# Gate products of the first branch placed among query projections, last heads and SSD preparation; second branch placed in recurrence and pooling

## The chip, the cores and the metric

The kernel runs on one core of a Trainium2 chip. The metric is the device time of one execution in microseconds. One more execution of the kernel was recorded by the hardware profiler; every row of a trace below is from it.

TensorE (PE) multiplies; a product of 128x128 weights with 512 columns is one matmul instruction. VectorE (DVE) and ScalarE (ACT) work element by element and read PSUM, where the products land. GpSimd (POOL) works element by element in SBUF. SyncE (SP) issues nearly all DMAs. The profile gives the granted clock of TensorE as a share of its 2.4 GHz level; 0.50 is the 1.2 GHz level.

## The reference, cut to what matters

One layer, 512 tokens, width 1024. Four mixers read the same normalised hidden state; the output of each goes through its own weights and is gated by a product of the hidden state.

```python
h = rmsnorm(x, g_mix[l])
u = h @ w_in[l]
c_q, c_kv, k_r, u_pool, z, xbc, dt, lru_g, lru_x, gates = jnp.split(u, pts, axis=-1)
y_a = mla_mixer(c_q, c_kv, k_r, cos, sin, ...)       # 8 heads, rotary part shared by the heads
y_b = pool_mixer(u_pool, w_pool[l], pool_scale[l])   # causal windows of 2, 4, 8, 16
y_c = ssd_mixer(z, xbc, dt, ...)                     # chunks of 128 tokens
y_d = rglru_mixer(lru_g, lru_x, ...)                 # recurrence over tokens
gates = jax.nn.sigmoid(gates.reshape(b, s, N_BRANCH, D_MODEL))
merged = (gates[:, :, 0] * (y_a @ w_branch[l, 0]) + gates[:, :, 1] * (y_b @ w_branch[l, 1])
          + gates[:, :, 2] * (y_c @ w_branch[l, 2]) + gates[:, :, 3] * (y_d @ w_branch[l, 3]))
x = x + merged @ w_out[l]
x = x + jnp.square(jax.nn.relu(rmsnorm(x, g_mlp[l]) @ w_ff1[l])) @ w_ff2[l]
x = x + (p[l] @ w_ple[l]) * jax.nn.sigmoid(rmsnorm(x, g_ple[l]) @ w_ple_gate[l])
return rmsnorm(x, g_final)
```

The four branches are called 0 (attention), 1 (pooling), 2 (SSD) and 3 (recurrence).

## The kernel before

**Products.** Every operand is split into a rounded part and a rest (`split`, `split_scaled`), and each product is three matmuls with float32r operands (`mm3`, lines 199 to 202). A projection (`proj`, line 292) of 8 blocks is 24 matmuls into one PSUM tile of tag m, of which there are three buffers. A product with a branch's own weights has 4 blocks, 12 matmuls.

**Weights.** They come in units, in the order of the list `UNITS` (lines 53 to 116): SP loads 128x1024 numbers, ACT makes the rounded part `wh` (line 169), DVE the rest `wl` (line 170). `unit()` keeps two units ahead; there are two raw and three split buffers.

**Order.** The kernel is written in program order, and a planner that simulates the engines while the program is built makes from it the instruction list of each engine. Program order is the priority; an instruction that the planner takes to be ready may be placed ahead of others. On the chip every engine works its list strictly in order. A tile has a tag with a fixed number of buffers (line 122: G1, G2, G3 16 each, T1 6, T2 8, T3 6, Z 4, X 8), and a new tile of a tag waits until an old one has been read for the last time.

**Stages around the change, in program order:**

- Line 431: a projection for the rotary key and dt, then three units of query weights (lines 443 to 452). Two of the six query tiles hold the rotary parts; `rotate` (line 421) reads such a PSUM tile six times on DVE, and writes two heads, the second by an addition on POOL (line 429). The others are copied by ACT (`head_pair`).
- Lines 453 to 467: key and value projections; lines 456 to 458 make eight masked copies of the rotated key.
- Lines 516 to 558: attention, one head per turn, the scores of the next head beside the weighting of this one. `split_head` (line 494) splits a head's key and query into four T1 tiles, the rounded part on ACT, the rest on POOL. After each of the first six heads stands one xBC projection (`xbc_tile`, line 483).
- Lines 561 to 578: `branch(n, j)` is gate product, tanh on ACT, product with the branch's weights, one DVE instruction, and for all branches but the first an addition on POOL into `merged[j]`. The tanh of the first branch lies in G3, of the others in T2.
- Lines 581 to 701: SSD. `branch(0, c)` stands after each of four chunks (line 689).
- Lines 717 to 741: four turns of the recurrence, `branch(0, 4 + i)` in each (line 722). Lines 747 to 758: four gelu turns. Lines 764 to 784: four pooling turns, in which POOL adds shifted copies and a matmul (line 783) mixes the result.
- Lines 789 to 796: branches 2, 1 and 3, eight times each; after branch 1 the residual x is loaded again (line 795). Then `merged` is split and the output projection follows (line 802).

Of the kernel before, what the change touches and what calls it, by code (L numbers as in the profile page):

```python
# [10 lines left out]
F32 = mybir.dt.float32  # L11
F32R = mybir.dt.float32r
# [5 lines left out]
P = 128  # L18
S = 512
# [37 lines left out]
def _unit(key, width):  # L57
    UIDX[key] = len(UNITS)
    UNITS.append((key, width))
# [4 lines left out]
for _i in range(4):  # L64
    _unit(("z", _i), 1024)
_unit(("krdt", 0), 576)
for _i in range(3):
    _unit(("uq", _i), 768)
_unit(("uk", 0), 1024)
_unit(("uv", 0), 1024)  # L70
for _i in (4, 5, 0, 1, 2, 3):
    _unit(("xbc", _i), 1024)
BR_ORDER = (0, 2, 1, 3)

UQ_ORDER = ((1, 0), (0, 0), (1, 1), (1, 2), (0, 1), (1, 3))


def _branch_units(n, j):
    _unit(("gate", n, j), 1024)
    if j % 2 == 0:  # L80
        _unit(("br", n, j // 2), 1024)


for _i in range(8):
    if _i >= 4:
        _unit(("lx", _i - 4), 1024)
    _branch_units(BR_ORDER[0], _i)
for _i in range(4):
    _unit(("lg", _i), 1024)
for _i in range(4):  # L90
    _unit(("pool", _i), 1024)
for _n in BR_ORDER[1:]:
    for _j in range(8):
        _branch_units(_n, _j)
for _i in range(8):
# [23 lines left out]
def trunk(tc, xT, pT, pos, par_d, cst_d, gfin, wblk_d, wpool_d, W, out, dbg=None):  # L119
# [4 lines left out]
    with ExitStack() as ctx:  # L124
# [12 lines left out]
        def A(tag, dt=F32, n="a"):  # L137
            return ap_.tile([P, S], dt, name=nm(n), tag=tag, bufs=TAGS[tag])
# [271 lines left out]
            zs.append(a)  # L410


        qh = [A("G1", F32, "qraw") for _ in range(H)]
        kh = [A("G1", F32, "kraw") for _ in range(H)]

# [5 lines left out]
        def rotate(ps, r0, dst, dst2=None):  # L421
            tmp, tmc = A("T3", F32, "rot"), A("T3", F32, "roc")
            m = r0 + 32
            dve.tensor_tensor(out=tmc[64:, :], in0=ps[r0:r0 + 64, :], in1=cosT[r0:r0 + 64, :], op=ALU.mult)
            dve.tensor_tensor(out=tmp[64:96, :], in0=ps[m:m + 32, :], in1=sinS[m:m + 32, :], op=ALU.mult)
            dve.tensor_tensor(out=tmp[96:, :], in0=ps[r0:m, :], in1=sinS[r0:m, :], op=ALU.mult)
            dve.tensor_tensor(out=dst[64:, :], in0=tmc[64:, :], in1=tmp[64:, :], op=ALU.add)
            if dst2 is not None:
                pool.tensor_tensor(out=dst2[64:, :], in0=tmc[64:, :], in1=tmp[64:, :], op=ALU.add)

        w = unit("krdt", 0)
        ps = proj(w, hh, KD, stride=72, m=72)
# [5 lines left out]
        for t in range(NT):  # L438
            pe.transpose(out=ps[:, t * 8:(t + 1) * 8], in_=kd[64:72, t * P:(t + 1) * P], identity=ident[64:72, 64:72])
        dtr = SM(32, "dtr")  # L440
        dve.tensor_tensor(out=heads(dtr, 8), in0=heads(ps[:, 0:32], 8),
                          in1=pc("dtb", 0, 8).unsqueeze(1).to_broadcast([P, NT, 8]), op=ALU.add)
        for u in range(3):
            w = unit("uq", u)
            for v in range(2):
                ps = proj(w, cq, 3, off=v * 384)
                a, i = UQ_ORDER[2 * u + v]
                if a:
                    head_pair(ps, i, qh)
                else:  # L450
                    for p in (2 * i, 2 * i + 1):
                        rotate(ps, (p % 2) * 64, qh[2 * p], qh[2 * p + 1])
        w = unit("uk", 0)
        for i in range(4):
            head_pair(proj(w, ckv, 2, off=i * 256), i, kh)
        for hd in range(H):
            dve.tensor_scalar(out=kh[hd][64:, :], in0=kro[64:, :], scalar1=cc("half", hd % 2, 1)[64:, :],
                              scalar2=None, op0=ALU.mult)
        w = unit("uv", 0)
        vv = []  # L460
        for t in range(NT):
# [29 lines left out]

        def split_head(src):
            h, l = A("T1", F32R, "hdh"), A("T1", F32R, "hdl")
            act.copy(out=h, in_=src)
            pool.tensor_tensor(out=l, in0=src, in1=h.bitcast(F32), op=ALU.subtract)
            return h, l

        def scores(q, k, qt):  # L500
            n = (qt + 1) * P
# [12 lines left out]
            return sm  # L514

        ya = []
        k_ = split_head(kh[0])
        q_ = split_head(qh[0])
        pr = [scores(q_, k_, qt) for qt in range(NT)]
        for hd in range(H):  # L520
            nxt = []
            po = PS("o")
            if hd + 1 < H:
                k_ = split_head(kh[hd + 1])
                q_ = split_head(qh[hd + 1])
            def weighted(kt, h, l):
                ro = (hd % 2) * 64
                vs = slice(hd * 64 - ro, hd * 64 + 64)
# [19 lines left out]
            pr = nxt  # L548
            if hd < 6:
                xbc_tile((4, 5, 0, 1, 2, 3)[hd])  # L550
            if hd % 2 == 0:
                yh, yl = A("G3", F32R, "yah"), A("G3", F32R, "yal")
                act.copy(out=yh[:64, :], in_=po[:64, :])
                dve.tensor_tensor(out=yl[:64, :], in0=po[:64, :], in1=yh[:64, :].bitcast(F32), op=ALU.subtract)
                ya.append((yh, yl))
            else:
                act.copy(out=yh[64:, :], in_=po[64:, :])
                dve.tensor_tensor(out=yl[64:, :], in0=po[64:, :], in1=yh[64:, :].bitcast(F32), op=ALU.subtract)


        yall = {0: ya}
        merged = [None] * 8
        bws = {}

        def branch(n, j):
            gw = unit("gate", n, j)
            if j % 2 == 0:
                bws[n] = unit("br", n, j // 2)
            pg = proj(gw, hh, KD)
            first = n == BR_ORDER[0]  # L570
            th = A("G3" if first else "T2", F32, "gth")
            act.activation(out=th, in_=pg, func=AF.Tanh, scale=0.5)
            pb = proj(bws[n], yall[n], 4, off=(j % 2) * S)
            dve.scalar_tensor_tensor(out=th, in0=th, scalar=1.0, in1=pb, op0=ALU.add, op1=ALU.mult)  # L574
            if first:
                merged[j] = th
            else:
                pool.tensor_tensor(out=merged[j], in0=merged[j], in1=th, op=ALU.add)  # L578


        dt = softplus(dtr, 32)
# [33 lines left out]
        for c in range(NT):  # L615
            ps = PS("t")
            for i in range(4):
                pe.transpose(out=ps[:, i * P:(i + 1) * P], in_=xbc[i][:, csl(c)], identity=ident)
            xt = A("T1", F32, "xt")
            act.copy(out=xt, in_=ps)  # L620
            xdt.append(A("G1", F32, "xdt"))
            xsd.append(A("G1", F32, "xsd"))
            dve.tensor_tensor(out=heads(xdt[c]), in0=heads(xt), in1=bc8(dt[:, c8(c)]), op=ALU.mult)
            pool.tensor_tensor(out=heads(xsd[c]), in0=heads(xt), in1=bc8(pc("dsk", 0, 8)), op=ALU.mult)
        btall = A("T1", F32, "bt")
        ps = PS("t")
        for c in range(NT - 1):
# [3 lines left out]
        for g in range(2):  # L631
            ps = PS("s")
            gs = slice(g * 64, g * 64 + 64)
            for c in range(NT):
                pe.matmul(ps[:, csl(c)], lhsT=xbc[4][gs, csl(c)], rhs=xbc[5][gs, csl(c)], start=True, stop=True)
            dve.tensor_tensor(out=heads(cbm[g], P), in0=heads(ps, P), in1=U.unsqueeze(1).to_broadcast([P, NT, P]),
                              op=ALU.mult)
        for c in range(NT):
            for g in range(2):
                e = A("G1", F32, "E")  # L640
# [3 lines left out]
                for j in range(4):  # L644
# [3 lines left out]
                pool.tensor_tensor(out=heads(e, P), in0=heads(e, P),  # L648
                                   in1=cbm[g][:, csl(c)].unsqueeze(1).to_broadcast([P, 4, P]), op=ALU.mult)
                G.append(e)  # L650

        R = [None]
        for c in range(NT - 1):
# [16 lines left out]
        for c in range(NT):  # L670
# [15 lines left out]
                dve.tensor_tensor(out=xsd[c], in0=y, in1=xsd[c], op=ALU.add)  # L686
            dve.tensor_tensor(out=zs[c], in0=xsd[c], in1=zs[c], op=ALU.mult)
            act.activation(out=y, in_=zs[c], func=AF.Square, accum_out=yssq[:, c:c + 1])
            branch(BR_ORDER[0], c)
        v = SM(NT, "v")  # L690
        dve.tensor_scalar(out=v, in0=yssq, scalar1=1.0 / (4 * 512), scalar2=EPS, op0=ALU.mult, op1=ALU.add)
        f = rsqrt(v, NT)
# [4 lines left out]
        for i in range(4):  # L697
            ps = PS("t")
            for c in range(NT):
                pe.transpose(out=ps[:, c * P:(c + 1) * P], in_=zs[c][:, i * P:(i + 1) * P], identity=ident)  # L700
            yc.append(split_scaled(ps, pc("snorm", i), "G1", "yc"))


        wba, wbi = A("T3", F32, "wba"), A("T3", F32, "wbi")
# [12 lines left out]
        for i in range(4):  # L717
            w = unit("lx", i)
            ps = proj(w, hh, KD)
            xc, e = A("G1", F32, "xc"), A("G1", F32, "le")  # L720
            conv(ps, lcw, pc("lcb", 0, 4), 4, i, xc)
            branch(BR_ORDER[0], 4 + i)
            pa, pi = PS("s"), PS("s")
            pe.matmul(pa, lhsT=wba[:, i * P:(i + 1) * P], rhs=xc, start=True, stop=True)
            pe.matmul(pi, lhsT=wbi[:, i * P:(i + 1) * P], rhs=xc, start=True, stop=True)
# [21 lines left out]
        for i in range(4):  # L747
# [7 lines left out]
            act.activation(out=t, in_=t, func=AF.Tanh, scale=GELU_C)  # L755
            dve.scalar_tensor_tensor(out=t, in0=t, scalar=1.0, in1=g, op0=ALU.add, op1=ALU.mult)
            dve.tensor_tensor(out=t, in0=t, in1=lus[i], op=ALU.mult)
            yd.append(split_scaled(t, 0.25, "G1", "yd"))


        wpl = A("T3", F32, "wpl")
        sync.dma_start(out=wpl, in_=wpool_d)
        yb = []
        for i in range(4):
            w = unit("pool", i)
            ps = proj(w, hh, KD)
# [12 lines left out]
                                     op0=ALU.mult, op1=ALU.subtract)  # L779
            dve.tensor_tensor(out=a[:, :n], in0=src[:, :n], in1=cc("rc", i * 16, n), op=ALU.mult)  # L780
            dve.tensor_tensor(out=a[:, :n], in0=a[:, :n], in1=u[:, :n], op=ALU.subtract)
            ps = PS("t")
            pe.matmul(ps, lhsT=wpl[:, i * P:(i + 1) * P], rhs=a, start=True, stop=True)
            yb.append(split_scaled(ps, pc("psc", i), "X", "yb"))

        yall.update({1: yb, 2: yc, 3: yd})


        for n in BR_ORDER[1:]:
            for j in range(8):  # L790
                branch(n, j)
            if n == 1:
                xres = [A("X", F32, "x") for _ in range(KD)]
                for k in range(KD):
                    sync.dma_start(out=xres[k], in_=xT[:, k, :])
        mg = [split_scaled(m, 0.5, "G1", "mg") for m in merged]


        def residual_in(g):
# [335 lines left out]
```

## Time and profile before

| | |
|---|---|
| median of 3 runs | 1002.74 us (1002.37 to 1002.94) |
| the profiled execution | 1005.16 us, of which its span 1003.1 us |
| busy in the span | PE 966.5 us, DVE 666.1, ACT 485.4, POOL 171.3 |
| mean granted TensorE clock | 0.989 |
| DMA | 96.97 MB, mean 97 GB/s |

Read first the busy times, then the same by stage with the granted clock, then what TensorE waited for, and last the timelines around the longest waits. A matmul's duration in the trace overlaps with the next; the distance from start to start is what it costs.

### The profile page before, as it was taken

Reading aid. Unit: us, or ns where it says so; the run is one execution under the profiler, and the core shown is the slowest. Engines: PE = TensorE matmul, PEld = TensorE weight load, DVE = VectorE, ACT = ScalarE, POOL = GpSimd, SP = SyncE. Lnnn points to the kernel's source line nnn. Section 1 sums busy time; section 2 is a strip of 40 time slices with the busy share of each in tenths; the row PEclk is TensorE's granted clock in tenths of the full one; section 3 lists DMA queues with packets and bytes.
Section 4 is the critical chain, followed back from the end, with each engine's and each line's share of the span. In section 5 each row is a group of like instructions: output and inputs, shape, how many; then the busy total and the mean of one; then the engine's idle time right before and its main releaser. Section 6 shows DMA issues by size and latency. Waiting matters only on the chain. (4 is left out here: it accounts for less than half of the span.)

```text
span 1003.1 us, 12054 instructions
## 1 busy us (share of the span) xinstructions
PE 966.5 (96%) x4389; PEld 787.6 (79%) x4389; DVE 666.1 (66%) x1140; ACT 485.4 (48%) x856; POOL 171.3 (17%) x127
## 2 busy tenths in 40 slices
PE   7997999899999899999999999999999999999996
PEld 5776788687777678888888888778887887888785
DVE  7769776657676743434342655897788689689636
ACT  6746786755367432222232434453543453466633
POOL 0003221133004351111121000423005005000021
PEclk9998999999999899999999999999999999999998
DMA  5422121042113223232532334433213404424002
GB/s 196 133 69 85 64 71 56 22 148 85 64 63 105 95 81 109 84 105 84 189 106 85 105 110 146 144 116 125 84 59 121 155 13 126 154 77 147 1 1 84
DMA packets 36475, 96.97 MB, mean 97 GB/s; under 512 B 4768, under 2 KB 4800, under 8 KB 36416
## 3 DMA queue, kind: packets, MB, share of 16 engines
q1 hardware_dynamic: 35472, 95.35, 28.9%
q10 hardware_dynamic: 944, 0.85, 0.3%
q8 instruction: 34, 0.56, 0.2%
q14 instruction: 25, 0.20, 0.1%
HBM read 94.01 MB, written 2.18 MB: 96 GB/s over the span
## 5 line engine op out<-in xcount | busy, mean ns | idle before, releaser
L170 DVE TENSOR_TENSOR wl<-wr,wh 128x1024 fp32r<-128x1024 f32 (+3 forms) x126 | 162.3, 1291 | 149.8 <-ACT wh L169 148.3
L169 ACT CAST wh<-wr 128x1024 fp32r<-128x1024 f32 (+3 forms) x126 | 128.7, 1023 | 251.9 <-PE psm L201 164.6
L200 PE MATMUL psm<-hh,wh 128*128 128x512 f32 (+1 forms) x408 | 163.5, 401 | 0.0
L201 PE MATMUL psm<-hl,wh 128*128 128x512 f32 (+1 forms) x408 | 161.4, 396 | 0.0
L202 PE MATMUL psm<-hh,wl 128*128 128x512 f32 (+1 forms) x408 | 160.7, 394 | 0.0
L202 PE MATMUL psm<-x2h,wl 128*128 128x512 f32 x256 | 100.0, 391 | 0.9 <-DVE wl L170 0.9
L200 PE MATMUL psm<-x2h,wh 128*128 128x512 f32 x256 | 99.9, 390 | 0.0
L201 PE MATMUL psm<-x2l,wh 128*128 128x512 f32 x256 | 99.9, 390 | 0.0
L201 PEld LDWEIGHTS psm<-hl,wh 128*128 128x128 f32 (+1 forms) x408 | 76.9, 188 | 18.3 <-issue 2.4
L200 PEld LDWEIGHTS psm<-hh,wh 128*128 128x128 f32 (+1 forms) x408 | 76.7, 188 | 18.5 <-issue 2.3
L202 PEld LDWEIGHTS psm<-hh,wl 128*128 128x128 f32 (+1 forms) x408 | 76.8, 188 | 18.0 <-issue 1.7
L185 DVE TENSOR_TENSOR wl<-b,wh 128x512 fp32r<-128x512 f32 x96 | 81.8, 898 | 2.5 <-ACT wh L184 2.5
L184 ACT CAST wh<-b 128x512 fp32r<-128x512 f32 x96 | 54.4, 618 | 56.0 <-PE pss L202 30.4
L865 POOL TENSOR_TENSOR t<-b,b 128x512 f32<-128x512 f32 x16 | 26.9, 1691 | 238.5 <-DVE xtok L856 136.4
L578 POOL TENSOR_TENSOR gth<-gth,gth 128x512 f32<-128x512 f32 x24 | 34.9, 1453 | 158.1 <-DVE gth L574 158.1
L202 PEld LDWEIGHTS psm<-x2h,wl 128*128 128x128 f32 x256 | 48.1, 188 | 11.6 <-DVE wl L170 1.8
L200 PEld LDWEIGHTS psm<-x2h,wh 128*128 128x128 f32 x256 | 48.1, 188 | 9.9
L201 PEld LDWEIGHTS psm<-x2l,wh 128*128 128x128 f32 x256 | 48.1, 188 | 9.8
L883 DVE SCALAR_TENSOR_TENSOR ffr<-psm,bc 128x512 f32<-128x512 f32 x32 | 21.9, 688 | 35.3 <-PE psm L202 32.1
L574 DVE SCALAR_TENSOR_TENSOR gth<-gth,psm 128x512 f32<-128x512 f32 x32 | 22.0, 687 | 16.2 <-PE psm L202 15.9
L987 POOL TENSOR_TENSOR xtok<-xtok,gf 128x512 f32<-128x512 f32 x7 | 9.0, 1290 | 134.1 <-ACT pth L986 134.1
L200 PE MATMUL psm<-pgh,xph 128*128 128x512 f32 (+1 forms) x72 | 26.6, 370 | 0.8 <-ACT xph L940 0.8
(398 smaller groups left out, 2105.4 us busy)
## 6 DMA issues: line engine op xcount, KB each, us to landing
wr<-W SPq DMA_DIRECT2D x114, 512.0 KB, 3.3
b<-W SPq DMA_DIRECT2D x64, 256.0 KB, 3.4
pgw<-W SPq DMA_DIRECT2D x16, 256.0 KB, 2.9
x<-xT SPq DMA_DIRECT2D x15, 256.0 KB, 6.6
wr<-W SPq DMA_DIRECT2D x8, 320.0 KB, 4.3
E<-acd SPq DMA_DIRECT2D x8, 256.0 KB, 6.2
out<-xtok SPq DMA_DIRECT2D x8, 256.0 KB, 2.3
wr<-W SPq DMA_DIRECT2D x3, 384.0 KB, 2.9
```

The costliest lines, as they stand in the source:

```text
L169: act.copy(out=hi[:, :n], in_=raw[:, :n])
L170: dve.tensor_tensor(out=lo[:, :n], in0=raw[:, :n], in1=hi[:, :n].bitcast(F32), op=ALU.subtract)
L184: act.copy(out=hi[:, c], in_=src)
L185: dve.tensor_tensor(out=lo[:, c], in0=src, in1=hi[:, c].bitcast(F32), op=ALU.subtract)
L200: pe.matmul(ps, lhsT=s_h, rhs=m_h, start=first, stop=False, **kw)
L201: pe.matmul(ps, lhsT=s_h, rhs=m_l, start=False, stop=False, **kw)
L202: pe.matmul(ps, lhsT=s_l, rhs=m_h, start=False, stop=last, **kw)
L574: dve.scalar_tensor_tensor(out=th, in0=th, scalar=1.0, in1=pb, op0=ALU.add, op1=ALU.mult)
L578: pool.tensor_tensor(out=merged[j], in0=merged[j], in1=th, op=ALU.add)
L865: pool.tensor_tensor(out=t1, in0=b12, in1=b11, op=ALU.subtract)
L883: dve.scalar_tensor_tensor(out=r, in0=ps, scalar=0.0, in1=rb, op0=ALU.max, op1=ALU.mult)
L987: (dve if last else pool).tensor_tensor(out=xt[t][hf][:, c], in0=xt[t][hf][:, c], in1=gf[:, hf, c], op=ALU.mult)
```

## The change

The first branch is taken apart into its gate product (`gate`) and the product with its weights (`project`). Gates (0,0) and (0,1) stand among the query projections, (0,2) and (0,3) after the last two heads, (0,4) behind the attention, (0,5) to (0,7) in the SSD preparation; their tanh lies in X or G1, not in G3. The SSD chunks keep the eight products. Branch 2 is spread over the recurrence, gelu and pooling turns (`MIXED`), and branch 3 goes ahead of branch 1. The rotation's second sum becomes a copy on ACT; a head's rest parts are made on DVE, and the masked key copy with them, head by head. The pooling matmul stands one turn later. x is loaded again after the split of `merged`. Other tags change to make room. The list of units follows the new order.

```diff
-for _i in range(3):
-    _unit(("uq", _i), 768)
+_unit(("gate", 0, 0), 1024)
+_unit(("uq", 0), 768)
+_unit(("uq", 1), 768)
+_unit(("gate", 0, 1), 1024)
+_unit(("uq", 2), 768)
...
-BR_ORDER = (0, 2, 1, 3)
+BR_ORDER = (0, 2, 3, 1)
...
+MIXED = {"lx": ((), (), (0,), (1,)), "lg": ((2,), (3,), (4,), (5,)), "pool": ((), (6,), (), (7,))}
...
+        yall = {}
+        merged = [None] * 8
+        gts, bws = {}, {}
+
+        def gate(n, j, tag="T2"):
+            pg = proj(unit("gate", n, j), hh, KD)
+            gts[n, j] = th = A(tag, F32, "gth")
+            act.activation(out=th, in_=pg, func=AF.Tanh, scale=0.5)
+
+        def project(n, j):
+            if j % 2 == 0:
+                bws[n] = unit("br", n, j // 2)
+            pb = proj(bws[n], yall[n], 4, off=(j % 2) * S)
+            th = gts.pop((n, j))
+            dve.scalar_tensor_tensor(out=th, in0=th, scalar=1.0, in1=pb, op0=ALU.add, op1=ALU.mult)
+            if n == BR_ORDER[0]:
+                merged[j] = th
+            else:
+                pool.tensor_tensor(out=merged[j], in0=merged[j], in1=th, op=ALU.add)
+
+        def branch(n, j):
+            gate(n, j)
+            project(n, j)
...
             if dst2 is not None:
-                pool.tensor_tensor(out=dst2[64:, :], in0=tmc[64:, :], in1=tmp[64:, :], op=ALU.add)
+                act.copy(out=dst2[64:, :], in_=dst[64:, :])
...
+        gate(0, 0, "X")
         for u in range(3):
+            if u == 2:
+                gate(0, 1, "X")
             w = unit("uq", u)
...
-        for hd in range(H):
-            dve.tensor_scalar(out=kh[hd][64:, :], in0=kro[64:, :], scalar1=cc("half", hd % 2, 1)[64:, :],
-                              scalar2=None, op0=ALU.mult)
...
-        def split_head(src):
-            h, l = A("T1", F32R, "hdh"), A("T1", F32R, "hdl")
-            act.copy(out=h, in_=src)
-            pool.tensor_tensor(out=l, in0=src, in1=h.bitcast(F32), op=ALU.subtract)
-            return h, l
+        def split_heads(hd):
+            dve.tensor_scalar(out=kh[hd][64:, :], in0=kro[64:, :], scalar1=cc("half", hd % 2, 1)[64:, :],
+                              scalar2=None, op0=ALU.mult)
+            return split(kh[hd], "T1", "hd"), split(qh[hd], "T1", "hd")
...
             if hd < 6:
                 xbc_tile((4, 5, 0, 1, 2, 3)[hd])
+            else:
+                gate(0, hd - 4, "G1")
...
+        yall[0] = ya
+        gate(0, 4, "G1")
...
-            xdt.append(A("G1", F32, "xdt"))
-            xsd.append(A("G1", F32, "xsd"))
+            xdt.append(A("G3", F32, "xdt"))
+            xsd.append(A("G3", F32, "xsd"))
...
+        gate(0, 5, "G1")
         btall = A("T1", F32, "bt")
...
+        gate(0, 6, "G1")
         for c in range(NT):
...
+        gate(0, 7, "G1")
...
             act.activation(out=y, in_=zs[c], func=AF.Square, accum_out=yssq[:, c:c + 1])
-            branch(BR_ORDER[0], c)
+            project(0, 2 * c)
+            project(0, 2 * c + 1)
...
-            xc, e = A("G1", F32, "xc"), A("G1", F32, "le")
+            xc, e = A("G3", F32, "xc"), A("G3", F32, "le")
             conv(ps, lcw, pc("lcb", 0, 4), 4, i, xc)
-            branch(BR_ORDER[0], 4 + i)
+            for j in MIXED["lx"][i]:
+                branch(2, j)
...
-            yd.append(split_scaled(t, 0.25, "G1", "yd"))
+            yd.append(split_scaled(t, 0.25, "G3", "yd"))
+            for j in MIXED["lg"][i]:
+                branch(2, j)
...
+        def mix(i):
+            ps = PS("t")
+            pe.matmul(ps, lhsT=wpl[:, i * P:(i + 1) * P], rhs=pds[i], start=True, stop=True)
+            h, l = A("Z", F32R, "ybh"), A("X", F32R, "ybl")
...
-            ps = PS("t")
-            pe.matmul(ps, lhsT=wpl[:, i * P:(i + 1) * P], rhs=a, start=True, stop=True)
-            yb.append(split_scaled(ps, pc("psc", i), "X", "yb"))
+            pds.append(a)
+            if i:
+                mix(i - 1)
+            for j in MIXED["pool"][i]:
+                branch(2, j)
+        mix(3)
...
-        for n in BR_ORDER[1:]:
+        for n in BR_ORDER[2:]:
             for j in range(8):
                 branch(n, j)
-            if n == 1:
-                xres = [A("X", F32, "x") for _ in range(KD)]
-                for k in range(KD):
-                    sync.dma_start(out=xres[k], in_=xT[:, k, :])
-        mg = [split_scaled(m, 0.5, "G1", "mg") for m in merged]
+        mg = []
+        for m in merged:
+            h, l = A("G1", F32R, "mgh"), A("G3", F32R, "mgl")
...
+        xres = [A("X", F32, "x") for _ in range(KD)]
+        for k in range(KD):
+            sync.dma_start(out=xres[k], in_=xT[:, k, :])
```

## Rows read from the trace of the kernel before

**Rows 1.** The page, busy times of the engines: us (share of the span) xinstructions.
```profile
PE 966.5 (96%) x4389; PEld 787.6 (79%) x4389; DVE 666.1 (66%) x1140; ACT 485.4 (48%) x856; POOL 171.3 (17%) x127
```

**Rows 2.** Busy time by stage: stretch, PE, weight load, DVE, ACT, POOL, clock, DMA.
```profile
72.00:105.00 33.00, 25.39 (x102) 19.66 (x101) 32.08 (x51) 17.91 (x30) 10.21 (x7) 0.90 0.25 80
105.00:174.00 69.00, 69.00 (x359) 58.10 (x359) 48.31 (x126) 53.20 (x120) 13.77 (x11) 1.00 0.21 68
174.00:203.00 29.00, 25.94 (x145) 19.51 (x144) 18.18 (x50) 21.67 (x58) 4.10 (x3) 0.94 0.12 37
...
264.00:308.00 44.00, 43.43 (x181) 32.88 (x179) 31.10 (x41) 29.38 (x45) 0.00 (x0) 1.00 0.25 84
...
338.00:350.00 12.00, 7.41 (x19) 4.95 (x18) 8.02 (x12) 4.07 (x7) 6.26 (x6) 0.72 0.27 88
350.00:600.00 250.00, 250.00 (x1099) 205.95 (x1098) 107.03 (x109) 76.76 (x99) 45.26 (x38) 1.00 0.31 105
```

**Rows 3.** Waits of PE, whole span: line, releaser, total us, times, longest.
```profile
PE psm L200 <- DVE rot L426: 4.9, 2, 3.6
PE pst L783 <- issue: 4.6, 1, 4.6
PE psm L200 <- DVE vl L283: 2.1, 1, 2.1
```

**Rows 4.** Timeline of PE, query projections: start, us, instruction, [idle before <-releaser].
```profile
90.79 0.77 PE L200 MATMUL psm<-lnh,wh 128*128 128x512 f32 x1 [3.64 <-DVE rot L426]
91.36 0.63 PE L201 MATMUL psm<-lnl,wh 128*128 128x512 f32 x1
...
96.47 0.55 PE L201 MATMUL psm<-lnl,wh 128*128 128x512 f32 x1
```

**Rows 5.** Timeline of PE at the first pooling matmul.
```profile
343.44 2.04 PE L783 MATMUL pst<-pd,wpl 128*128 128x512 f32 x2 [4.59 <-issue]
344.50 1.42 PE L201 MATMUL psm<-hl,wh 128*128 128x512 f32 x1
345.71 0.63 PE L202 MATMUL psm<-hh,wl 128*128 128x512 f32 x1
```

**Rows 6.** PE by line and form, 105 to 174 us: count, busy us, mean ns.
```profile
L200 PE MATMUL psm<-hh,wh 128*128 128x512 f32 x64 | 25.3, 396 | 0.0
...
L200 PE MATMUL pss<-hdh,hdh 128*128 128x512 f32 x6 | 2.5, 411 | 0.0
```

**Rows 7.** Three helper lines over the whole span: count, ns min/median/max, first and last start.
```profile
L497 POOL TENSOR_TENSOR hdl<-kraw,hdh x8: 1281/1302/2100, 95.8 to 174.8; 128x512 fp32r<-128x512 f32 x8
L457 DVE TENSOR_SCALAR kraw<-kro,cst x8: 487/492/1520, 94.4 to 100.4; 64x512 f32<-64x512 f32 x8
L283 DVE TENSOR_TENSOR hl<-hn,hh x8: 681/684/693, 39.1 to 49.3; 128x512 fp32r<-128x512 f32 x8
```

**Rows 8.** Timeline of DVE, 82 to 177 us.
```profile
82.68 2.28 DVE L427 TENSOR_TENSOR qraw<-roc,rot 64x512 f32<-64x512 f32 x2
...
85.08 1.22 DVE L170 TENSOR_TENSOR wl<-wr,wh 128x1024 fp32r<-128x1024 f32 x1
86.42 0.69 DVE L424 TENSOR_TENSOR roc<-psm,cosT 64x512 f32<-64x512 f32 x1
...
90.95 2.23 DVE L170 TENSOR_TENSOR wl<-wr,wh 128x1024 fp32r<-128x1024 f32 x1
...
176.03 1.45 DVE L489 SCALAR_TENSOR_TENSOR xbc<-xth,xbc 128x512 f32<-128x512 f32 x1
```

**Rows 9.** Timeline of ACT at the first pooling turn.
```profile
338.44 0.57 ACT L768 COPY pu<-psm 128x512 f32<-128x512 f32 x1
```

**Rows 10.** Timeline of POOL in the rotation.
```profile
90.81 1.27 POOL L429 TENSOR_TENSOR qraw<-roc,rot 64x512 f32<-64x512 f32 x1 [0.87 <-DVE rot L426]
```

**Rows 11.** The reload of x, instructions and landing.
```profile
L795 SPq DMA_DIRECT2D x<-xT x8: 328/430/1155, 486.4 to 490.1; - x8
...
DMA to landing us min/median/max: 3.0/5.8/6.9
```

More of the change, by code (lines that the diff above doesn't have):

```diff
@@ L81, in _branch_units @@
         _unit(("br", n, j // 2), 1024)
[L84 to L87, printed above, removed]
+for _i in range(2, 8):
+    _unit(("gate", 0, _i), 1024)
 for _i in range(4):
[L89 to L92, printed above, removed]
+    _unit(("br", 0, _i), 1024)
+for _n in ("lx", "lg", "pool"):
+    for _i in range(4):
+        _unit((_n, _i), 1024)
+        for _j in MIXED[_n][_i]:
+            _branch_units(2, _j)
+for _n in BR_ORDER[2:]:
     for _j in range(8):
@@ L516, in trunk @@
         ya = []
-        k_ = split_head(kh[0])
-        q_ = split_head(qh[0])
+        k_, q_ = split_heads(0)
         pr = [scores(q_, k_, qt) for qt in range(NT)]
@@ L523, in trunk @@
             if hd + 1 < H:
-                k_ = split_head(kh[hd + 1])
-                q_ = split_head(qh[hd + 1])
+                k_, q_ = split_heads(hd + 1)
             def weighted(kt, h, l):
@@ L558, in trunk @@
                 dve.tensor_tensor(out=yl[64:, :], in0=po[64:, :], in1=yh[64:, :].bitcast(F32), op=ALU.subtract)
[L561 to L578, printed above, removed]
+        yall[0] = ya
+        gate(0, 4, "G1")
         dt = softplus(dtr, 32)
@@ L701, in trunk @@
             yc.append(split_scaled(ps, pc("snorm", i), "G1", "yc"))
+        yall[2] = yc
         wba, wbi = A("T3", F32, "wba"), A("T3", F32, "wbi")
@@ L757, in trunk @@
             dve.tensor_tensor(out=t, in0=t, in1=lus[i], op=ALU.mult)
-            yd.append(split_scaled(t, 0.25, "G1", "yd"))
+            yd.append(split_scaled(t, 0.25, "G3", "yd"))
+            for j in MIXED["lg"][i]:
+                branch(2, j)
+        yall[3] = yd
         wpl = A("T3", F32, "wpl")
         sync.dma_start(out=wpl, in_=wpool_d)
-        yb = []
+        yb, pds = [], []
+        def mix(i):
+            ps = PS("t")
+            pe.matmul(ps, lhsT=wpl[:, i * P:(i + 1) * P], rhs=pds[i], start=True, stop=True)
+            h, l = A("Z", F32R, "ybh"), A("X", F32R, "ybl")
+            act.activation(out=h, in_=ps, func=AF.Identity, scale=pc("psc", i))
+            dve.scalar_tensor_tensor(out=l, in0=ps, scalar=pc("psc", i), in1=h.bitcast(F32), op0=ALU.mult, op1=ALU.subtract)
+            yb.append((h, l))
         for i in range(4):
@@ L781, in trunk @@
             dve.tensor_tensor(out=a[:, :n], in0=a[:, :n], in1=u[:, :n], op=ALU.subtract)
-            ps = PS("t")
-            pe.matmul(ps, lhsT=wpl[:, i * P:(i + 1) * P], rhs=a, start=True, stop=True)
-            yb.append(split_scaled(ps, pc("psc", i), "X", "yb"))
-        yall.update({1: yb, 2: yc, 3: yd})
-        for n in BR_ORDER[1:]:
+            pds.append(a)
[4 more added lines that the diff above has]
+        mix(3)
+        yall[1] = yb
+        for n in BR_ORDER[2:]:
             for j in range(8):
                 branch(n, j)
-            if n == 1:
-                xres = [A("X", F32, "x") for _ in range(KD)]
-                for k in range(KD):
-                    sync.dma_start(out=xres[k], in_=xT[:, k, :])
-        mg = [split_scaled(m, 0.5, "G1", "mg") for m in merged]
+        mg = []
+        for m in merged:
+            h, l = A("G1", F32R, "mgh"), A("G3", F32R, "mgl")
+            act.activation(out=h, in_=m, func=AF.Copy, scale=0.5)
+            dve.scalar_tensor_tensor(out=l, in0=m, scalar=0.5, in1=h.bitcast(F32), op0=ALU.mult, op1=ALU.subtract)
+            mg.append((h, l))
+        xres = [A("X", F32, "x") for _ in range(KD)]
+        for k in range(KD):
+            sync.dma_start(out=xres[k], in_=xT[:, k, :])
         def residual_in(g):
```

## The prediction

> **What bounds the kernel now.** I read the page's busy times first, then the busy time and granted clock by stage, then TensorE's waits, and last the timelines around the longest of them. TensorE (PE) is busy 966.5 of 1003.1 us [rows 1]. From 350 to 600 us it never stops: 1099 products, nearly all of 512 columns, in 250 us, 0.227 us each, at granted clock 1.00 [rows 2], which is the 2.4 GHz level. The change gives PE no arithmetic and takes none, so it can only win back the time in which PE stands still or runs at the lower level. What of that lies within its reach is in three stretches [rows 2]:
>
> A, 72 to 105 us (query projections): 25.39 of 33 us busy, 7.6 idle, clock 0.90, while VectorE (DVE) is busy 32.08. The named waits are 4.9 us for the rotation's last read of a PSUM tile and 2.1 for the split of v [rows 3]. The longest, 3.64 us, is followed by products that start 0.43 us apart (1.2 GHz), from 91.36 to 96.47 us [rows 4]: thirteen, with 0.2 us lost on each, and 0.3 on the one before them, 2.9. A holds 7.6 + 2.9 = 10.5 us.
>
> B, 174 to 203 us (last two heads): 25.94 of 29 busy, clock 0.94 [rows 2]. 3.1 us are idle; a mean of 0.94 means 12% of 29 us at the low level, 3.5 us, half of it lost, 1.8. B holds 4.9 us.
>
> D, 338 to 350 us (first pooling matmul): 4.6 us idle [rows 3], then the low level: the pair of pooling passes takes 1.06 us to the next start, where the next gap is 1.21 instead of 0.23, and then 9 gaps are 0.43 [rows 5]. Against two passes in some 0.45 us that is 0.6 + 1.0 + 1.8 = 3.4. D holds 8.0 us.
>
> Together 23.4 us. The attention between A and B has no idle PE (69 of 69 us), and 264 to 308 us (recurrence) only 0.6 us [rows 2].
>
> **The planner.** The written order is only a priority. From 105 to 174 us there are 64 first passes with the hidden state [rows 6], 8 to a product, so 8 products: the six xBC tiles and two gates that stand in the text only after the attention. So fill is taken forward already, where a buffer and a weight are there. In B it isn't: the gate's tanh needs a G3 tile, and 8 of v and 8 of the attention's output take all 16.
>
> **Part by part.** *Gates (0,0) and (0,1) in A, tanh in X.* Each is 24 products, 24 x 0.227 = 5.4 us of PE that wait for nothing of DVE but one weight split (1.2 us). They are taken from later, so no work is added. PE waits for DVE's backlog there, and 10.9 us of PE against 2.4 of DVE let it catch up. DVE also sheds six of the eight masked copies of the rotated key (0.49 us unhindered, 1.52 at worst [rows 7]), now made head by head. I take 7.6 of 10.5 back and leave 2.9, since the rotation still holds one of three PSUM buffers for some 4.2 us (six reads of 0.7 [rows 8]). Bounds 0 (the first rival) and 10.5.
>
> *The rotation's second sum, GpSimd (POOL) to ScalarE (ACT).* Four POOL additions go; four copies come, 0.57 us each by another copy of 512 columns [rows 9], 2.3 us on an engine busy 17.91 of 33 us here [rows 2]. Beside the POOL addition at 90.81 [rows 10] a weight split on DVE took 2.23 us, where another took 1.22 [rows 8]. Eight DVE instructions are longer beside POOL, from the second of the pair at 82.68 (0.69 alone, 2.28 for the pair) to the one at 176.03 [rows 8], each by 0.3 to 1.03 us, 6.8 in sum.
>
> *Head splits, POOL to DVE.* 16 subtractions of 1.28 us or more leave POOL, 16 of 0.684 [rows 7] join DVE: 10.9 us, against at most 6.8 back from that hindrance. Per head DVE gets 2 x 0.684 + 0.49 = 1.9 us. It is busy 48.3 of 69 us while six heads are scored [rows 2, 6]: 11.5 us a head, 8.1 of it busy, 10.0 after. That fits, with less slack; also the rotated key now lives through all heads and leaves T1 five of its six buffers. The cover is PE's xBC and gate products. I take 1.0 us of new waits; bounds 15.2 (8 x 1.9, no cover) and a gain of 6.8 (all of the hindrance on the path).
>
> A rule of the Trainium skill speaks against these two parts: Perfetto Trace Analysis, Optimizing Scalar/DVE Operations, says that GpSimd and VectorE share an SBUF read port, so that shifting work between them may not help. The long rows above agree that the two hinder each other. By the rule the sum stays as it is, since no gain is booked on them.
>
> *Gates (0,2) to (0,7), tanh in G1.* Two stand in the last heads, one right behind, three in the SSD preparation; G1 is freed as the raw heads are split. Two are 10.9 us of PE without a wait, against 4.9 lost in B. I take 4.0 back, bounds 0 and 4.9. The products with the first branch's weights follow in the SSD chunks, 8 x 12 x 0.227 = 21.8 us of fill.
>
> *Branch 2 between recurrence and pooling.* The first two recurrence turns lose the branch beside them. A turn is then 24 x 0.227 + 4 passes of 0.43 = 7.2 us of PE. Four turns with four branches had DVE busy 31.1 and ACT 29.4 of 44 us [rows 2], 7.8 and 7.3 a turn; without the branch (1.5 weight splits and a sum on DVE, 1.5 casts and a tanh on ACT, some 2.4 us each) it is 5 to 5.4: PE stays the longest. I take 1.0 us for the two turns; bounds 0 and 2 x (5.4 + 5.0 - 7.2) = 6.4, both engines one after the other. The gelu turns get a branch (36 products, 8.2 us) each, the pooling two. Now the first pooling input is copied at 338.44 [rows 9], though its product ended 5.4 us before PE stopped at 338.85 [rows 5], near 333.4: ACT waits in order for the gelu chain, which is behind. Eight us more of PE per turn take that away. The matmul also stands one pooling tile later in the text, but the trace shows it after the second tile's product already, so that alone gives nothing. Copy, POOL and DVE then need some 5 us against a product of 5.4. I take 6.0 of 8.0 back, bounds 2 and 8.
>
> *Reload of x behind all branches.* SP's eight loads, 5.8 us each to landing, move from 486 us [rows 11], where they lie beside products, to the output projection. Two find a buffer at once, four wait for the last branch's operands, two for the first merged tiles; weight loads queue behind them on SP. The first sum needs x 5.4 us after the projection begins, and three PSUM buffers give 16. I take 0, bounds 0 and 5.8, one landing laid open. The changed order of the branches costs nothing by itself: the same products in another row.
>
> **Sum:** 7.6 + 4.0 + 6.0 - 1.0 - 1.0 = 15.6 us. The profiled execution is 1005.16 us, 1003.1 of span and 2.1 around it, so the span should be 987.5. The median shown is 1002.74, 0.24% under the profiled one; taken from it, the time is 987.1 us.
>
> **Rivals.** *The buffers, not the engine (16%).* The gates use the same three PSUM buffers as the projections; while the rotation holds one and ACT is late with another, PE stops before a gate as it did before a projection. For: the 3.64 us wait was for a buffer. Against: a gate's buffer needs a single tanh. A gives 0, D only 4: 4.0 + 4.0 - 2.0 = 6 us, 996.7. The Trainium skill's Perfetto Trace Analysis, Matmuls, wants independent groups to rotate through different banks so that reading one overlaps the next; by it A would stay as it is.
>
> *DVE becomes the pace of the heads (12%).* If each head grows by its 1.9 us and fill runs out, 15.2 us lie open in the attention; B gives nothing, A 5 and D 4 (DVE is late there too), the recurrence takes 1: 1002.74 + 15.2 - 8 = 1010. It decides where more than 8 of the 15.2 us lie open. For: DVE goes from 70% to 87% there. Against: PE has no wait in these heads now, and six gates stand behind as fill.
>
> *The hole moves (10%).* Fill is spent early. The recurrence turns (6.4) and x (5.8) pay back most, and D gives only 2: 1002.74 - 7.6 - 4.0 - 2.0 + 12.2 = 1001.3.
>
> **How the numbers follow.** The forecast has 62%, its own range 979 (all 23.4 won) to 994; buffers 16%, heads 12%, moved hole 10%. Leaving out the heads and most of the moved hole, the range is 979 to 1001. About 0.2% is what a measurement of this kernel tells from no change, so faster is below 1000.7. Faster: 62 + 16 + 3 = 81%; same: 6 of the moved hole and 2 of the heads, 8%; slower: 10 + 1 = 11%.
>
> **What would show it.** A: no wait over 2 us for the rotation, clock 1.00 from 72 to 120 us. B: products with the hidden state between the last heads' transposes, no stretch at the low level. Heads: scored no more than 12 us apart. D: no idle PE over 2 us before a pooling matmul. Output projection: no wait for x. It is wrong if PE waits in the attention for head splits on DVE, or if the end of SSD or the first recurrence turns show new gaps of several us.

## The result and the profile after

The changed kernel takes 981.92 us (980.05 to 982.21, four runs) against 1002.84 us (1002.37 to 1004.88, four runs): 0.9774 of the kernel before, 95% interval 0.9757 to 0.9791, 20.9 us less. In two later comparisons it took 982.01 and 981.99 us, so the experiments below can be read against 982.0. The kernel before drifts more, from 1002.84 to 1005.61 us beside them, so the gain is 20.9 to 23.6 us. The profiled execution is 982.21 us with a span of 980.4 us; the span of before was 1003.1.

From the page of the changed kernel, the span, the busy times and the granted clock in 40 slices:

```profile
span 980.4 us, 12002 instructions
...
PE 954.9 (97%) x4389; PEld 782.4 (80%) x4389; DVE 661.4 (67%) x1156; ACT 489.4 (50%) x860; POOL 138.8 (14%) x107
...
PEclk9999999999999999999999999999999999999998
```

TensorE has the same 4389 products as in [rows 1], and of the three slices with a clock under 0.9 that the page of before has, only the last is left, the end of the program. Line numbers of the changed kernel are higher: the three passes of a product are lines 208 to 210, the rotation's last read 459, the head copies 451, the pooling matmul 790.

Busy time by stage (stretch, PE, weight load, DVE, ACT, POOL, clock, DMA share, GB/s). The stages are those of [rows 2], but they lie elsewhere: the query projections begin later, since a gate stands before them, and the attention is longer, since gates lie in it.

```profile
72.00:110.00 38.00, 34.32 (x152) 27.01 (x151) 32.28 (x59) 23.71 (x39) 0.00 (x0) 1.00 0.30 105
110.00:206.00 96.00, 96.00 (x499) 80.95 (x498) 67.92 (x171) 72.89 (x162) 0.00 (x0) 1.00 0.20 67
206.00:230.00 24.00, 22.17 (x136) 17.86 (x135) 13.71 (x27) 14.45 (x35) 5.10 (x4) 1.00 0.28 88
...
264.00:308.00 44.00, 44.00 (x193) 33.52 (x192) 34.10 (x58) 27.50 (x43) 2.57 (x2) 1.00 0.23 76
308.00:350.00 42.00, 42.00 (x187) 34.79 (x186) 26.34 (x28) 20.99 (x28) 16.36 (x10) 1.00 0.34 113
350.00:578.00 228.00, 228.00 (x1000) 187.29 (x999) 99.86 (x112) 74.38 (x97) 43.83 (x40) 1.00 0.32 106
```

From 72 to 578 us two stretches with idle TensorE are left, 3.7 us in the query projections (before 7.6) and 1.8 us at the end of the attention (before 3.1), and nowhere does it run at the low level. The recurrence, gelu and pooling turns have none. The waits of TensorE (line, releaser, total us, times, longest), those of the two stretches:

```profile
PE psm L208 <- ACT kraw L451: 2.3, 2, 1.5
PE psm L208 <- DVE rot L459: 1.4, 2, 1.1
...
PE pst L567 <- DVE ptl L571: 0.9, 1, 0.9
...
PE psm L208 <- DVE gth L435: 0.6, 1, 0.6
```

The rotation's 4.9 us of [rows 3] are 1.4, the 2.1 for the split of v and the 4.6 for the pooling matmul are gone; 2.3 us for the copy of key heads on ACT are new. The four pooling matmuls, in the timeline of TensorE (start, us, instruction; idle time before would stand in brackets), follow without a gap, where [rows 5] had 4.59 us:

```profile
372.57 1.02 PE L790 MATMUL pst<-pd,wpl 128*128 128x512 f32 x2
...
384.13 1.02 PE L790 MATMUL pst<-pd,wpl 128*128 128x512 f32 x2
```

### The profile page after: what moved, and what is told of

Its sections match the earlier page's. It is cut to its first block, busy times and chain, and to the rows that moved or that the text cites. A ratio compares the mean times of both kernels' runs of the same rounds, so it can differ in the third digit from the quotient of the medians.

```text
span 980.4 us, 12002 instructions
## 1 busy us (share of the span) xinstructions
PE 954.9 (97%) x4389; PEld 782.4 (80%) x4389; DVE 661.4 (67%) x1156; ACT 489.4 (50%) x860; POOL 138.8 (14%) x107
## 4 chain that ended last, share of the span: by engine, by line
PE 81%; DVE 13%; ACT 2%; issue 2%; DMA 2%; ACTq 0%; DVEq 0%
PE psm L208 21%; PE psm L210 21%; PE psm L209 21%; DVE wl L193 4%; PE pss L208 3%; PE pss L209 3%; PE pss L210 3%; DVE xtok L894 2%; DVE wl L178 1%; PE pst L567 1%; PE pst L209 1%; PE pst L208 1%; PE pso L210 1%; PE pso L208 1%; PE pso L692 1%
## 5 line engine op out<-in xcount | busy, mean ns | idle before, releaser
L178 DVE TENSOR_TENSOR wl<-wr,wh 128x1024 fp32r<-128x1024 f32 (+3 forms) x126 | 157.6, 1254 | 112.2 <-ACT wh L177 105.3
L208 PE MATMUL psm<-hh,wh 128*128 128x512 f32 (+1 forms) x408 | 161.5, 396 | 0.3 <-DVE rot L459 0.3
L193 DVE TENSOR_TENSOR wl<-b,wh 128x512 fp32r<-128x512 f32 x96 | 84.1, 922 | 1.8 <-ACT wh L192 1.6
L638 POOL TENSOR_TENSOR xsd<-xt,par 128x512 f32<-128x512 f32 x4 | 5.5, 1392 | 224.5 <-ACT xt L634 224.5
```

What stands on the lines that cost most here:

```text
L178: dve.tensor_tensor(out=lo[:, :n], in0=raw[:, :n], in1=hi[:, :n].bitcast(F32), op=ALU.subtract)
L193: dve.tensor_tensor(out=lo[:, c], in0=src, in1=hi[:, c].bitcast(F32), op=ALU.subtract)
L208: pe.matmul(ps, lhsT=s_h, rhs=m_h, start=first, stop=False, **kw)
```

## The experiments

The theory was that independent products in the stretches with late operands are the gain (fill). The rivals were that the work taken off GpSimd, the buffers, or the later pooling matmul are. Each kernel is the changed one with the edit shown, unless it says otherwise.

### Gates (0,0) and (0,1) out of the query projections

```diff
-        gate(0, 0, "X")
         for u in range(3):
-            if u == 2:
-                gate(0, 1, "X")
...
             else:
+                gate(0, hd - 6, "X")
                 gate(0, hd - 4, "G1")
```

The list of units follows.

> The changed kernel with one part undone: gates (0,0) and (0,1) stand behind the last two heads and no longer among the query projections. Fill theory: the stretch of the query projections, which held 10.5 us of idle and low-clock time before and holds 3.7 us of waits after the change, gets 5 to 8 us back, 987 to 990 us against 981.9 of the changed kernel. Rival (it was the work taken off GpSimd and the key copies taken off VectorE that freed the stretch): the waits there stay under 5 us and the time is 980 to 984 us.

Measured: 984.83 us (984.59 to 986.55), 2.8 us over the changed kernel: between the two expectations, so neither holds alone. (The changed kernel did not run beside this one, nor beside the two below without the mixing and with late gates. By the ratios to the kernel before, 0.9803, 0.9825 and 0.9859 against 0.9774, the three edits cost 2.9, 5.1 and 8.5 us.) Its busy time from 70 to 102 us, where the query projections now are, and the waits there:

```profile
70.00:102.00 32.00, 25.39 (x111) 19.18 (x110) 30.55 (x57) 22.60 (x39) 0.00 (x0) 1.00 0.28 95
```

```profile
PE psm L206 <- DVE rot L457: 3.5, 2, 2.3
PE psm L206 <- ACT kraw L449: 2.4, 2, 1.5
```

The stretch has 6.6 us of idle time and the clock at 1.00. The kernel before had 7.6 us there and lost 2.9 more at the low level, 10.5; the changed one has 3.7. So without the gates 3.9 us of the 6.8 are still won: its longest wait is 2.3 us, not 3.64, and no low clock follows it, which is 2.9 of the 3.9. The gates themselves are worth the other 2.9 us, as the time says too. What shortens the wait without them shows in VectorE's timeline of this run:

```profile
82.76 1.29 DVE L458 TENSOR_TENSOR qraw<-roc,rot 64x512 f32<-64x512 f32 x2
...
92.78 2.90 DVE L523 TENSOR_SCALAR kraw<-kro,cst 64x512 f32<-64x512 f32 x7
```

With no GpSimd addition beside them, two sums of the rotation take 1.29 us, where they took 2.28 [rows 8], and the last read of the next PSUM tile begins at 89.05 us, 0.9 earlier than before. That is most of the 1.36 us by which the wait is shorter. The masked key copies have no part in it: the planner takes all eight forward into this stretch, seven of them at 92.78 us, and before the change, too, they came after the longest wait (94.4 to 100.4 us against 90.79 [rows 7, rows 4]). That the GpSimd additions are the cause is read from these rows; a kernel without them and otherwise as before was not run.

### No branch 2 between the turns

```diff
-MIXED = {"lx": ((), (), (0,), (1,)), "lg": ((2,), (3,), (4,), (5,)), "pool": ((), (6,), (), (7,))}
+MIXED = {"lx": ((), (), (), ()), "lg": ((), (), (), ()), "pool": ((), (), (), (0, 1, 2, 3, 4, 5, 6, 7))}
```

> The changed kernel with branch 2 whole behind the pooling turns, so that recurrence, gelu and pooling turns have no branch beside them; the later pooling matmul stays. Fill theory: the idle time before a pooling matmul and the low clock behind it come back (8.0 us before the change), and the recurrence loses a little, 988 to 992 us. Rival (the matmul one turn later is what helped): no idle time over 2 us before a pooling matmul, 980 to 984 us.

Measured: 987.36 us (986.35 to 989.23), 5.4 us over the changed kernel. Its waits from 300 to 345 us, and the busy time from 326 to 344 us:

```profile
PE pst L790 <- issue: 2.3, 1, 2.3
PE psm L208 <- ACT pu L800: 2.0, 1, 2.0
```

```profile
326.00:344.00 18.00, 13.70 (x48) 9.55 (x48) 13.53 (x21) 7.13 (x11) 10.30 (x12) 0.91 0.35 113
```

All eight products of branch 2 stand in the fourth pooling turn in this kernel. Idle time and a low clock are back before the first pooling matmul: 4.3 us, and a mean clock of 0.91. The time is just under the range of the fill theory, and well over the rival's. The wait is shorter than the 4.59 us of before and split in two: a projection now waits for the late copy of the pooling input on ACT, and the matmul for the rest of the chain.

### Each pooling matmul in its own turn

```diff
-            if i:
-                mix(i - 1)
+            mix(i)
...
-        mix(3)
```

> The changed kernel with each pooling matmul in its own pooling turn again, as before the change; branch 2 stays mixed in. Theory 1 (the branch between the turns removes the delay, the later place gives nothing): within 1 us of the changed kernel, no idle TensorE over 1 us before a pooling matmul. Theory 2 (without branch 2 the changed kernel still had 4.3 us of idle time there, so the later place covers part): 2 to 4 us above it, with an idle time before the matmuls of the third and fourth tile.

Measured: 981.75 us (981.5 to 981.97), beside 981.99 us of the changed kernel on the same chip. From 300 to 500 us TensorE waits for nothing in its trace. Theory 1 holds: with branch 2 between the turns the later place gives nothing.

### Gates (0,2) to (0,7) right before their products

```diff
-            else:
-                gate(0, hd - 4, "G1")
...
-        gate(0, 4, "G1")
...
-            project(0, 2 * c)
-            project(0, 2 * c + 1)
+            for j in (2 * c, 2 * c + 1):
+                if c:
+                    gate(0, j, "G1")
+                project(0, j)
```

Gates (0,5) to (0,7) go in the same way, and in the list of units each gate stands beside the branch weights that it is used with.

> The changed kernel with gates (0,2) to (0,7) written right before their products in the SSD chunks, their tanh still in G1. Buffer theory: the planner takes a gate forward wherever its buffer is free, so the last heads are filled all the same, 980 to 985 us. Rival (the written position matters): the last heads have no gate beside them, idle and low-clock time of 3 to 5 us come back, 985 to 988 us.

Measured: 990.93 us (989.84 to 992.47), 8.9 us over the changed kernel, more than either expectation; the low clock that the rival expected did not come. Busy time over the heads in this kernel, and two forms of TensorE there (count | busy us, mean ns):

```profile
109.00:204.00 95.00, 89.39 (x488) 73.35 (x488) 70.87 (x186) 72.82 (x173) 0.00 (x0) 1.00 0.16 51
```

```profile
L210 PE MATMUL psm<-hh,wh 128*128 128x512 f32 x56 | 22.1, 394 | 0.0
...
L210 PE MATMUL pss<-hdh,hdh 128*128 128x512 f32 x8 | 3.2, 404 | 0.0
```

And the same two forms in the changed kernel, from 110 to 206 us:

```profile
L208 PE MATMUL psm<-hh,wh 128*128 128x512 f32 x95 | 37.4, 393 | 0.0
...
L208 PE MATMUL pss<-hdh,hdh 128*128 128x512 f32 x7 | 2.8, 407 | 0.0
```

With the gates written late, 56 first passes lie between the heads, seven products: the six xBC tiles and one gate, though G1 can hold all six gates, as it does in the changed kernel. With the gates written early it is 95, nearly twelve. So the planner took only one of them forward on its own; the written place, and with it the place in the list of units, decides. Whether the order of the weights or that of the buffers holds them back was not separated. 5.6 us of the heads are idle. Between the two profiled executions, 988.4 and 980.4 us, 4.5 of the 8.0 us are idle time (30.0 against 25.5 over the whole span); most of the rest lies in greater distances from start to start between the small products, those of scores, weighting and transposes, which count as busy.

The second form gives the pace: 8 heads scored in 95 us without fill, 11.9 us a head, 7 in 96 us with it, 13.7 us. In the first TensorE waits, in the second it is busy for all of the 96 us. So in the changed kernel TensorE itself sets the pace of the heads.

### The sums on GpSimd again

```diff
-                act.copy(out=dst2[64:, :], in_=dst[64:, :])
+                pool.tensor_tensor(out=dst2[64:, :], in0=tmc[64:, :], in1=tmp[64:, :], op=ALU.add)
...
-            return split(kh[hd], "T1", "hd"), split(qh[hd], "T1", "hd")
+            out = []
+            for src in (kh[hd], qh[hd]):
+                h, l = A("T1", F32R, "hdh"), A("T1", F32R, "hdl")
+                act.copy(out=h, in_=src)
+                pool.tensor_tensor(out=l, in0=src, in1=h.bitcast(F32), op=ALU.subtract)
+                out.append((h, l))
+            return out
```

> The changed kernel with the rest parts of the head splits and the rotation's second sum on GpSimd again; the key copies stay head by head. Fill theory: TensorE is fed by independent products, so it doesn't matter who does them, 980 to 984 us. Rival 1 (shared port: 6.8 us of hindered VectorE time come back on the path): 986 to 989 us. Rival 2 (VectorE paces the heads after the change): faster, under 980 us.

Measured: 979.53 us (979.0 to 980.26), faster than the changed kernel and in the range of rival 2. Its reason does not hold, though: TensorE has no idle time in the heads of the changed kernel, and the splits alone give nothing (below). Rival 1 fails: VectorE is hindered again, the eight key copies take 5.38 us in the profile instead of 3.30, but not on the path. Since a gain of this size is near what runs differ by, both were run again side by side, five rounds each.

> The changed kernel beside the next one on the same chip: 0.974 to 0.981 of the kernel before.

> The version with the head splits and the rotation's second sum on GpSimd, beside the changed kernel on the same chip. If its 2.9 us were real: 2 to 4 us below the changed kernel. If they came from the chip: within 1 us of it.

Measured: 981.99 us (980.82 to 982.24) for the changed kernel, 979.15 us (978.11 to 980.16) with the sums on GpSimd: 2.8 us less, and the ranges don't touch. That is 0.9738 of the kernel before, interval 0.9722 to 0.9754, the fastest version of this study. Its waits from 72 to 240 us:

```profile
PE psm L208 <- DVE gth L435: 1.5, 1, 1.5
PE psm L208 <- DVE rot L459: 1.4, 2, 1.1
PE psm L208 <- ACT kraw L451: 0.5, 2, 0.3
```

The wait for the key copies on ACT has gone from 2.3 to 0.5 us. To see which of the two edits does it, each was made alone, next to the changed kernel:

> The changed kernel itself, as the reference for the runs on the same chip. Every theory: 0.974 to 0.981 of the kernel before.

> The changed kernel with only the rotation's second sum on GpSimd again; the head splits stay on VectorE. With both on GpSimd the kernel was 0.9745 of the kernel before, against 0.9774 of the changed one, some 2.9 us. Theory 1 (the four copies on ScalarE delay the key copies that the projections wait for, 2.3 us of waits in the changed kernel): most of it comes from here, 2 to 3 us below the changed kernel on the same chip. Theory 2 (the splits on VectorE lengthen the path at the end of the attention): less than 1 us below it.

> The changed kernel with only the head splits' rest parts on GpSimd again; the rotation's second sum stays a copy on ScalarE. Theory 1 (the copies on ScalarE cost the time): less than 1 us below the changed kernel on the same chip. Theory 2 (the splits on VectorE cost it): 2 to 3 us below it.

Measured: 982.01 us for the changed kernel (981.33 to 983.04), 980.93 us with the rotation's sum on GpSimd (980.1 to 981.76), 982.09 us with the splits there (981.33 to 983.45). In the first the wait for the key copies is nearly gone, in the second it stays; the lines of the one and of the other:

```profile
PE psm L208 <- ACT kraw L451: 0.2, 1, 0.2
```

```profile
PE psm L208 <- ACT kraw L451: 2.3, 2, 1.5
```

So the copies on ACT cost some 1.1 us (the ranges of the runs just overlap, but the wait goes with them) and the splits by themselves nothing, while both together cost 2.8. The two are not additive, and what the remaining 1.7 us are stays open. Theory 1 had the sign and the place right, but half of the size. How four copies of 0.6 us make TensorE wait shows in the changed kernel, on ACT and, last, on TensorE:

```profile
97.96 0.62 ACT L462 COPY qraw<-qraw 64x512 f32<-64x512 f32 x1 [1.07 <-DVE qraw L460]
99.94 0.62 ACT L462 COPY qraw<-qraw 64x512 f32<-64x512 f32 x1 [1.36 <-DVE qraw L460]
100.58 3.58 ACT L451 COPY kraw<-psm 64x512 f32<-64x512 f32 x6
```

```profile
101.82 0.50 PE L208 MATMUL psm<-lnh,wh 128*128 128x512 f32 x1 [1.46 <-ACT kraw L451]
```

A copy reads the sum that VectorE has still to make. ACT stands idle 1.07 and 1.36 us for it, and the copies of the key heads, which would free the PSUM tiles, stand behind.

### The gates alone

The changed kernel with both sums on GpSimd and no branch 2 between the turns, both edits as above.

> Of the change, the gates of branch 0 in their new places with the buffers they need, the key copies head by head, the later pooling matmul and the new branch order; branch 2 isn't mixed in, and both sums are on GpSimd as before. If the parts add up: 0.9774 - 0.0029 + 0.0051 = 0.9796 of the kernel before, some 20.5 us under it, with 4 us of idle time at the pooling matmuls. If mixing and the move off GpSimd depend on each other: over 0.983 or under 0.977.

Measured: 985.82 us (984.42 to 986.67), 0.9803 (0.9787 to 0.9819) of the kernel before, where adding up gave 0.9796: the parts add up within the interval. It is 19.8 us below the kernel before in this comparison (1005.61 us), so the gates with their places, buffers and order of weights carry most of the change. The new order of branches 1 and 3 and the other tags are in this kernel as in all the others; they were not tested by themselves. Its waits at the pooling matmul, 3.1 us where 4 were expected:

```profile
PE psm L208 <- ACT pu L806: 2.0, 1, 2.0
...
PE pst L796 <- issue: 1.1, 1, 1.1
```

### An attempt at more

Both sums on GpSimd, gate (0,1) between the second rotary tile and the last query tile, and gate (2,0) behind gate (0,7):

```diff
-            if u == 2:
-                gate(0, 1, "X")
...
                         rotate(ps, (p % 2) * 64, qh[2 * p], qh[2 * p + 1])
+                    if u == 2:
+                        gate(0, 1, "X")
...
         gate(0, 7, "G1")
+        gate(2, 0)
```

> An attempt at a faster version: both parts on GpSimd again, gate (0,1) between the second rotary query tile and the last query tile, so that it runs while the rotation holds its PSUM tile, and gate (2,0) written with the last gates of the SSD preparation. Fill theory: the 1.1 us wait for the rotation and the 1.5 us wait before the first branch products go, 2 to 3 us below the version with both on GpSimd, 0.9715 to 0.973 of the kernel before. Rival (the wait moves to the next PSUM tile): no more than 1 us below it, 0.9735 to 0.975.

Measured: 983.06 us (981.86 to 985.11), 0.9786 of the kernel before: slower than the version that it starts from, and outside both expectations. Its waits from 72 to 300 us:

```profile
PE pss L210 <- DVE m L550: 2.1, 1, 2.1
PE psm L210 <- ACT kraw L454: 1.6, 1, 1.6
PE psm L210 <- ACT ych L298: 1.6, 1, 1.6
PE psm L210 <- DVE gth L437: 1.5, 1, 1.5
PE psm L210 <- DVE rot L462: 0.3, 1, 0.3
```

The wait for the rotation went as meant, 1.4 to 0.3. In its place the value projection waits 1.6 us and the first scores 2.1, and after that wait the granted clock is 0.50 for over 3 us from about 111 us on; and with one product of branch 2 gone from the recurrence, the branch's first product waits 1.6 us for its operand. The wait before the first branch products, 1.5, is still there. The hole moved. Which of the two moved gates costs how much was not separated.

## Why the prediction was right, and where not

The time, 981.92, lies in the range of 979 to 1001 and in the forecast's own of 979 to 994. The gain was 20.9 us where 15.6 were forecast. Step by step:

**What bounds the kernel** held. Most of the gain, 17.9 of 22.7 us of span, is idle and low-clock time of TensorE in the stretches A, B and D, and no product was added or taken.

**A, 7.6 forecast.** 6.8 us came back (10.5 to 3.7). The size was right, the cause half right, so the size was in part luck: the step gave all of it to the gates' fill, and with the gates taken away again 3.9 us stay won. They go with VectorE instructions that are no longer hindered by GpSimd, on which the sum booked nothing. The six key copies that VectorE was to shed were not shed: all eight still run in the stretch, after the rotation, since the planner takes them forward.

```profile
99.83 3.30 DVE L528 TENSOR_SCALAR kraw<-kro,cst 64x512 f32<-64x512 f32 x8
```

The sign written for A, no wait over 2 us and the clock at 1.00, is there.

**B, 4.0 forecast.** The idle time went from 3.1 to 1.8 us and the 1.8 us of low clock are gone, 3.1 together. The reason in the paragraph on the planner was too narrow: it blamed the full G3 alone. With their tanh in G1, but the gates written late, only one was taken forward. And the step's price was taken from the idle time of one stretch; undoing the placement cost 8.9 us, more than twice what was booked. The idle time of that run lies between 161 and 209 us, the length of four heads and not of two.

**D and the turns, 6.0 less 1.0 forecast.** All 8.0 us came back and the recurrence lost nothing: TensorE is busy 44 of 44 us from 264 to 308. Undoing the mixing gave 5.4 us, near the 5.0 booked. That the later place of the matmul gives nothing was right with branch 2 between the turns; without it, it was not tested by itself.

**The head splits, 1.0 us of cost, and the copies on ACT, free.** The heads from 110 to 206 us have no idle TensorE, so there the 1.0 was too much. But the two moves together cost 2.8 us, and 1.1 of it is in the copies that the step held to be covered on an engine busy 17.91 of 33 us [rows 2]. The failure: it looked at that engine's mean, not at what stands in its queue. The copies wait there for VectorE's sum, before the key heads' copies, which free the PSUM buffers that the next projections wait for; that is the 2.3 us wait. The sum kept no gain from moving work off GpSimd, and with the gates in place there was none: the splits alone changed nothing (982.09 against 982.01). By that the trace agrees with the Trainium skill (Perfetto Trace Analysis, Optimizing Scalar/DVE Operations), where shifting work between GpSimd and VectorE may not help.

**The reload of x, 0 forecast.** VectorE's sums with x wait for TensorE alone:

```profile
DVE x L842 <- PE psm L210: 16.2, 7, 4.0
```

**The sum.** In the spans the gain is 22.7 us: 6.8 in A, 3.1 in B, 8.0 in D and 0.6 in the recurrence make 18.5. The medians show 20.9, since the profiled execution of before was 2.3 us over its median. Some 4 us of span remain that the four terms don't hold, and the forecast had no term for them. By the distances from start to start, some 2 of them are in small products of SSD, which stand closer after the change (the twelve `pst<-R,xbc` take 2.52 us in all, before 3.73); that was not tested by itself.

**The rivals.** The buffers (997): A did win, though not all; what is left there are just such waits for a PSUM buffer, 1.4 for the rotation and 2.3 for ACT. The heads at DVE's pace (1010): the heads do lie 13.7 us apart, beyond the 12 that the prediction set as its sign, but not for DVE, which is busy 67.9 of 96 us, 71% and not 87%, part of it since the key copies, 0.49 of its 1.9 us a head, run earlier. Without fill they lie 11.9 apart, splits on DVE and all. The sign was badly chosen: fill itself puts the heads farther apart. The moved hole (1001): it did not come with the change, but it is what stopped the attempt at more.

## What to carry to other kernels

Where TensorE waits for operands in one stage and has independent products in another, write these products, and their weights in the order of loading, into the stage that waits: a planner that may take them forward took one of six by itself here (8.9 us). Before work is moved to an engine with idle time on the mean, look at what that engine's queue owes at that place: four copies on a half idle ACT cost some 1.1 us since they waited for VectorE before the copies that free PSUM. And after the large holes are closed, moving two single products only moved the waits here.

## What the runs showed of the hardware that was not expected

GpSimd is slowed by VectorE as well as the other way round. Its shifted addition over 510 columns took 2.07 us at 343 us in the kernel before, where VectorE split weights beside it; in the changed kernel the same addition, with VectorE idle, takes half of that. The timeline of GpSimd before, that of VectorE before, and that of GpSimd after:

```profile
343.34 2.07 POOL L773 TENSOR_TENSOR pa<-pa 128x510 f32<-128x510 f32 x1
```

```profile
343.29 1.22 DVE L170 TENSOR_TENSOR wl<-wr,wh 128x1024 fp32r<-128x1024 f32 x1
```

```profile
373.01 1.03 POOL L805 TENSOR_TENSOR pa<-pa 128x510 f32<-128x510 f32 x1
```
